# Two-layer hybrid decoder: shift sums on VectorE, a new pace for the modulation rows, and two FFN panels held back into attention

## The chip, the core and the metric

The kernel runs on one core of one Trainium2 chip. The metric is device time in microseconds (us) from one launch, the median of several runs. Instructions go to five engines: TensorE (PE in the profile, with weight loads as PEld), VectorE (DVE), ScalarE (ACT), GpSimd (POOL) and SyncE (SP), each of which works through its own queue in order.

## The reference

The input is x of 1024 tokens by 1024 channels and a conditioning vector c. Each layer makes six modulation vectors of 1024 values from c; each normalised input is scaled and shifted by two of them, and each sub-layer's output is scaled by a third before it is added to x.

```python
cond = silu(c)
for i in range(2):
    sh1, sc1, g1, sh2, sc2, g2 = split(cond @ ada_w[i] + ada_b[i], 6)
    h = rmsnorm(x, norm_mix_g[i]) * (1 + sc1) + sh1
    x = x + g1 * (rglru_mixer(h) if i == 0 else dsa_mixer(h))
    h = rmsnorm(x, norm_ffn_g[i]) * (1 + sc2) + sh2
    x = x + g2 * (square(relu(h @ ffn_w1[i])) @ ffn_w2[i])
```

Layer 0's mixer projects h to 1280 channels of a convolution branch and 1280 of a gate branch, runs a gated linear recurrence in 5 blocks of 256 channels over time, and projects back. Layer 1's mixer is attention of 16 heads with one shared key and value; an indexer of 8 heads chooses the 256 best keys for each query. The FFN is 1024 to 4096 to 1024.

## The kernel before

Activations lie with channels on the 128 partitions and tokens along the free axis, in two halves of 512 tokens, h = 0 and 1; a half of x is 8 tiles of 128 x 512. Every large product is made of three matmuls (`mm3`, L351 to L353): weights and activations are each split into a rounded part and a remainder (wh and wl, hh and hl). ScalarE rounds the weights (L328), and GpSimd or VectorE takes the remainder (L334). Layer 0's last eight FFN weight panels are written back to HBM in split form when half 0 uses them, and are only loaded for half 1.

The program text is one long list. A planner of the framework puts instructions on the engines' queues by its own estimate of when each is ready, with the place in the program as priority, so an instruction can stand in its queue ahead of one that the program names earlier. Buffers are given out by the same planner.

**Start (`startup`, L496).** For each of 8 channel blocks kt the 128 columns of the first scale and of the first shift are needed (`A0`, `S0`). Two raw tiles of `ada_w` hold both. `cols` (L555) makes the scale sums on TensorE by 8 tiny matmuls of one output column, each of which stands in the trace as two records. For kt under `NS` = 4 it makes the shift sums in the same way; for kt of 4 and above `mac` (L542) makes them on VectorE, as 8 operations of 128 x 128, which TensorE turns (L565) and VectorE reduces (L567); L568 then writes S0. The block's normalised input follows (L97 to L100), and with it the first 18 matmuls of the mixer. `lru_params` (L386) makes some 30 tiny constants of the recurrence; the program calls it in `mixer0` after the second convolution.

**Layer 0's mixer (`mixer0`, L609).** After the start it goes through a list of steps, `plan`: "c20" is the convolution (`conv`) of block 2 for half 0, "g" the gate, "l" the recurrence (`lru`), "o010" the output projection of blocks 0 and 1 for half 0. After every step `pump` takes one item from a list of small work, `fill`. Its items are the other modulation rows: `ada` (L430) gives for each row 8 `mac` items, of two VectorE operations on 128 x 512 each (L456 for the first, L458 for the others), and a `fin` that turns and reduces the sums (L465, L466). Each `mac` also starts the load of the next one's data, on ScalarE's queue (L441). The row for g1, `ada(0, 2)`, comes first; its `fin` is the eighth step of the plan, ahead of "o010", the first that needs it. Two items are pumped before the mixer. `nB` (L1321) and `nA` (L1325) make a normalised input in one step: `bc` (L84) broadcasts 1/rms over the partitions into a bank of PSUM, and `apply` runs L102 on VectorE, L103 on ScalarE and L104 on VectorE for each of 8 blocks. Output projections take one PSUM tile (`ps`, four of them) per block of 128 channels, which VectorE empties (L728).

**From layer 0 to layer 1 (`run`, L1403 on).** Half 1's second eight FFN panels run in a loop: `f1` of panel p+1, then `f2` of panel p, 8 PSUM tiles of 6 matmuls, each added to x by VectorE (L174). Between them stand blocks of layer 1 for half 0: keys, values and indexer, the scores, and `q_group(0, 0)`, the first eight heads' queries. After the last panel come half 1's norm (`stat`, L71, and `bc`), and `q_group(0, 1)` with half 1's `apply` in its gaps. Then `attention(0)` starts, which at certain points takes steps from a generator, `background`, at a given `rate` per point: half 1's keys, values and indexer, and the first half of the output projection. What is left of it when attention ends runs bare (`finish`).

Of the kernel before, what the change touches and what calls it, by code (L numbers as in the profile page):

```python
# [19 lines left out]
KT = 8  # L20
# [182 lines left out]
class Trunk:  # L203
# [292 lines left out]
    def startup(self, pool, norm, normb):  # L496


        nc, V, A = self.nc, self.nc.vector, self.nc.scalar
        NS = 4  # L500
        A0 = self.mod[0, 1] = self.const.tile([P, KT], FT, name="mod01")
        S0 = self.mod[0, 0] = self.const.tile([P, KT], FT, name="mod00")

# [10 lines left out]
        norm.bc(keep=self.nlong())  # L514
        b1 = self.small([P, KT], "mb", 1)
        V.scalar_tensor_tensor(b1, self.ada_b(0, 1), 1.0, self.gmix(0), op0=OP.add, op1=OP.mult)
        pd = [self.pd(), self.pd()]
        acc = [pd[0][:, 0], pd[0][:, 1], pd[1][:, 0], pd[1][:, 1], self.ps(), self.ps()]
        wt, ad = {}, {}
# [22 lines left out]
        def mac(kt):  # L542

            if kt < NS:
                return
# [9 lines left out]
        def cols(kt):  # L555
            ps = self.ps()
            for e in range(2 if kt < NS else 1):
                for k in range(KT):
# [4 lines left out]
            t = ps[:, 1:2]  # L563
            if kt >= NS:
                nc.tensor.transpose(ps[:, P:2 * P], sums[kt], self.ident)  # L565
# [43 lines left out]
    def mixer0(self, hx, g1, tail, first, plan):  # L609
# [21 lines left out]
        def conv(u, h, pss=None):  # L631
            pss = pss or proj(wcols(u * 256), h)
            for j in range(2):
                f = 2 * u + j
                y = self.tmp("xc")
                A.activation(y, pss[j], AF.Identity, bias=self.convb(f), scale=self.convw(3, f))
                if h == 0:
                    A.copy(halo[:, f], pss[j][:, HT - 3:HT])
                for k in range(3):
                    d = 3 - k  # L640
                    V.scalar_tensor_tensor(y[:, d:], pss[j][:, 0:HT - d], self.convw(k, f), y[:, d:],  # L641
                                           op0=OP.mult, op1=OP.add)
                if h:
                    V.tensor_tensor(y[:, 0:3], y[:, 0:3], edge[:, f], op=OP.add)
                yh, yl = self.tileR(), self.tileR()
                A.copy(yh, y)
                G.tensor_tensor(yl, y, yh.bitcast(FT), op=OP.subtract)
                xc[u, j], xcs[u, j] = y, (yh, yl)
# [83 lines left out]
        conv(0, 0, first[0])  # L732
        gate(0, 0, first[1])
        conv(1, 0, first[2])
        self.lru_params()
        for k, step in enumerate(plan):
            if callable(step):
                step()
            else:
                us = [int(u) for u in step[1:-1]]  # L740
                {"c": conv, "g": gate, "l": lru, "o": oproj}[step[0]](us if step[0] == "o" else us[0], int(step[-1]))
                if step == "c40":
                    edges()
            self.pump()


    def l1_consts(self):
# [510 lines left out]
    def run(self):  # L1258
        tc = self.tc
        mod = self.mod = {}  # L1260
        N = {}
        hm, hf = {}, {}

        def pool(st, name, bufs):
            return st.enter_context(tc.tile_pool(name=name, bufs=bufs))

        def sqs(key):
            def tail(h, m):
                if m == 0:
                    N[key, h] = Norm(self, h)  # L1270
                N[key, h].sq(m)
            return tail

        turns = []
# [5 lines left out]
        def run(gen):  # L1280
            for _ in gen:
                pass
# [8 lines left out]
        def turn_next():  # L1291
            for g in turns.pop(0):
                g()

        def flush():
            while turns:
                turn_next()
# [3 lines left out]
        NJ = 8  # L1301
# [11 lines left out]
        F = FFN(self, 0, None, hf)  # L1313
        with ExitStack() as st:
            self.tp = pool(st, "tmp0", 18)
            macs, fin = self.ada(0, 2)
            self.fill += macs
            self.ada_fill([(0, 4, self.gffn(0)), (0, 3), (0, 5)])
            self.pump(2)

            def nB():  # L1321
                N["m0", 1].bc()
                hm[1] = N["m0", 1].apply(mod[0, 1], mod[0, 0])

            def nA():  # L1325
                N["f0", 0].bc()
                hf[0] = N["f0", 0].apply(mod[0, 4], mod[0, 3])

            def stat0():
                N["f0", 0].stat()  # L1330

            def f1a():
                self.drain()
                F.load1(0)
                F.f1(0, 0)

            def f1b():
                def bcB():
                    N["f0", 1].bc()
                    hf[1] = N["f0", 1].apply(mod[0, 4], mod[0, 3])  # L1340

                F.load1(1)
                F.f1(1, 0, mid={4: lambda: N["f0", 1].stat(), 6: bcB})

            plan = [lambda: self.second(), "g10", "l00", "c20", "l10", "g20", "c30", fin, "o010", "l20", "g30", "c40",
                    "l30", "g40", nB, "o20", "l40", "c01", "g01", "o340", "l01", "c11", stat0, "g11", "c21", "l11",
                    "g21", "c31", "o011", "l21", "g31", "c41", "l31", "g41", nA, "o21", "l41", f1a, "o341", f1b]
            self.mixer0(hm, lambda: mod[0, 2], sqs("f0"), first, plan)
            self.drain()


            F.g2, F.tail = mod[0, 5], tail
            self.ada_fill([(1, 1, self.gmix(1)), (1, 0), (1, 2), (1, 4, self.gffn(1)), (1, 3), (1, 5)])
            F.load2(0, 0)
            f2 = F.f2_steps([0], 0)
            for _ in range(4):
                next(f2)
            F.f1(0, 1), F.f1(1, 1)
            F.load2(0, 1)
            run(f2)  # L1360
            F.f2([0], 1)
            for p in range(NJ):
                if p:
                    F.load2(p, 0), F.load2(p, 1)
                    for h in range(2):
                        F.f2([p], h)
                if p + 2 < NJ:
                    F.load1(p + 2)
                    F.f1(p + 2, 0), F.f1(p + 2, 1)
            self.drain()  # L1370
            F.twice = range(NJ, F.NP)
            F.single(0, NJ)
# [6 lines left out]
        with ExitStack() as st:  # L1379
            self.tp = pool(st, "tmpt", 12)  # L1380
            self.hidpool = self.tp
            self.qi, self.qiT, self.qT, self.sc = {}, {}, {}, {}
            hm[0] = []
            def start():
                N["m1", 0].bc()
                hm[0] += N["m1", 0].apply(mod[1, 1], mod[1, 0])
                self.l1_consts()

            def idx(t):
                flush()  # L1390
                for f in self.idx_steps(t):
                    f()
                self.fill += self.topk_steps(t)

            N["m1", 0].stat()
            self.npump = 2
            F.load1(NJ)
            F.f1(NJ, 1)
            start()
            blocks = [lambda: (steps(self.kv_steps(0, hm[0]), 4), steps(self.qi_steps(0, hm[0]), 4)),  # L1400
                      lambda: (idx(2), idx(3)), lambda: None, lambda: None, lambda: None,
                      lambda: (flush(), run(self.q_group(0, 0, hm[0], turns)))]
            for p in range(NJ, F.NP):  # L1403
                if p + 1 < F.NP:
                    F.load1(p + 1)
                    F.f1(p + 1, 1)
                F.load2(p, 0), F.load2(p, 1)
                F.f2([p], 1)
                if blocks:
                    blocks.pop(0)()  # L1410
            self.hidpool = None
            N["m1", 1].stat()
            flush()


            self.lo = [1, 1, 0]
            q1 = self.q_group(0, 1, hm[0], self.late_turns)
            hm[1] = []
            next(q1)
            N["m1", 1].bc(keep=self.rstd_b)  # L1420
            for k in range(KT):
                hm[1].append(N["m1", 1].apply1(k, mod[1, 1], mod[1, 0]))
                next(q1)
            run(q1)
            self.drain()

            def background():
                self.second_half()
                yield from feed(self.kv_steps(1, hm[1]), 2)
                yield from feed(self.qi_steps(1, hm[1]), 2)  # L1430
                self.reload(0)
                while self.units < 8 + 1:
                    yield
                yield from self.proj_out(0, mod[1, 2], 0)

            self.banks(True)
            self.bg, self.rate = background(), 1
            self.attention(0)
            self.finish()
            flush()  # L1440
        with ExitStack() as st:
# [27 lines left out]
            F = FFN(self, 1, mod[1, 5], hf)  # L1469
# [7 lines left out]
            f2 = F.f2_steps([F.NP - 2, F.NP - 1], 0)  # L1477
# [75 lines left out]
```

## Time and profile before

| | |
|---|---|
| time, median of 3 runs | 2583.12 us (2579.7 to 2590.5) |
| time of the profiled execution | 2589.09 us |
| its span, first to last instruction | 2587.3 us |
| TensorE busy | 2449.9 us, 95% of the span |
| VectorE busy | 1500.7 us, 58% |
| ScalarE busy | 1234.9 us, 48% |
| GpSimd busy | 965.9 us, 37% |
| mean granted TensorE clock | 0.974 of full |
| DMA | 342.53 MB, 132 GB/s over the span |

The profiled execution took 1.8 us more than its span. Busy time of TensorE is modelled for pipelined matmuls, so a slice in which it is full can still run at the lower of its two clocks. In a row of the timeline or of a view of waits the bracket at the end says how long the engine sat idle before that instruction and what released it.

### The profile page before, as it was taken

What the parts mean: (1) busy time and instruction counts of PE and PEld (TensorE: products, weight loads), DVE (VectorE), ACT (ScalarE), POOL (GpSimd) and SP (SyncE); (2) the same over time, 40 slices, a digit from 0 to 9 for tenths busy, and PEclk for the clock granted to TensorE, in tenths of its full rate; (3) what the DMA queues carried; (4) which work ended last, traced back from release to release, by engine and by line L of the source; (5) the groups of instructions that cost most, each with busy time, mean ns of one, the idle gap of its engine ahead of it and who ended that gap; (6) DMA issues with size and microseconds to landing.
All of it is one profiled execution on the core that took longest, in us unless ns stands there. A gap on an engine that the chain in (4) does not pass through costs nothing. (4 is left out here: it accounts for less than half of the span.)

```text
span 2587.3 us, 31024 instructions
## 1 busy us (share of the span) xinstructions
PE 2449.9 (95%) x11014; PEld 1976.0 (76%) x11014; DVE 1500.7 (58%) x2802; ACT 1234.9 (48%) x2187; POOL 965.9 (37%) x575
## 2 busy tenths in 40 slices
PE   8779899998999999999997999999998999999999
PEld 7567678776788888888776877888887777788887
DVE  3677965678934421366677877565558876321112
ACT  3455555632122142235546767768743974433322
POOL 3455421122221234230136932222225994344442
PEclk8889999999999999999998999999999999999999
DMA  6556466336611277744431431232330104322231
GB/s 207 197 183 202 164 220 227 123 110 212 207 49 49 98 249 284 279 165 175 147 117 31 172 102 57 91 97 82 105 131 8 34 25 144 111 96 92 88 101 62
DMA packets 212285, 342.53 MB, mean 132 GB/s; under 512 B 19658, under 2 KB 123298, under 8 KB 212130
## 3 DMA queue, kind: packets, MB, share of 16 engines
q1 hardware_dynamic: 183184, 295.29, 33.8%
q10 hardware_dynamic: 28946, 45.27, 5.3%
q8 instruction: 86, 1.41, 0.2%
q14 instruction: 69, 0.57, 0.1%
HBM read 274.97 MB, written 65.54 MB: 132 GB/s over the span
## 5 line engine op out<-in xcount | busy, mean ns | idle before, releaser
L334 POOL TENSOR_TENSOR wl<-raw,wh 128x1024 fp32r<-128x1024 f32 (+2 forms) x233 | 569.3, 2451 | 1102.3 <-ACT wh L328 1075.0
L328 ACT CAST wh<-raw 128x1024 fp32r<-128x1024 f32 (+2 forms) x296 | 305.5, 1035 | 599.9 <-PE ps L352 237.9
L351 PE MATMUL ps<-a,wh 128*128 128x512 f32 x1152 | 463.2, 405 | 20.3 <-DVE a L728 10.8
L352 PE MATMUL ps<-a,wh 128*128 128x512 f32 x1152 | 460.7, 400 | 1.3 <-POOL a L710 1.1
L353 PE MATMUL ps<-a,wl 128*128 128x512 f32 x1152 | 459.0, 399 | 0.8 <-DMA wl<-part 0.8
L351 PE MATMUL pd<-a,wh 128*128 128x512 f32 x1072 | 430.4, 402 | 18.8 <-DVE xc L641 14.2
L352 PE MATMUL pd<-a,wh 128*128 128x512 f32 x1072 | 430.8, 402 | 5.6 <-DVE a L100 3.6
L353 PE MATMUL pd<-a,wl 128*128 128x512 f32 x1072 | 429.9, 401 | 0.0
L174 DVE SCALAR_TENSOR_TENSOR a<-ps,mod,a 128x512 f32<-128x512 f32 x352 | 260.0, 747 | 262.3 <-PE ps L353 261.5
L351 PEld LDWEIGHTS ps<-a,wh 128*128 128x128 f32 x1152 | 219.4, 191 | 76.7 <-DVE a L728 11.4
L352 PEld LDWEIGHTS ps<-a,wh 128*128 128x128 f32 x1152 | 219.5, 191 | 55.3 <-POOL a L710 3.4
L353 PEld LDWEIGHTS ps<-a,wl 128*128 128x128 f32 x1152 | 219.1, 190 | 54.6 <-DMA wl<-part 1.6
L351 PEld LDWEIGHTS pd<-a,wh 128*128 128x128 f32 x1072 | 203.8, 190 | 69.9 <-issue 15.9
L352 PEld LDWEIGHTS pd<-a,wh 128*128 128x128 f32 x1072 | 204.8, 191 | 57.4 <-DVE a L100 4.6
L353 PEld LDWEIGHTS pd<-a,wl 128*128 128x128 f32 x1072 | 204.6, 191 | 49.3
L1147 POOL TENSOR_SCALAR s<-s,rr 128x128 f32<-128x128 f32 (+7 forms) x128 | 225.4, 1776 | 33.3 <-DVE rr L1145 30.1
L351 PE MATMUL ps<-hid,wh 128*128 128x512 f32 x512 | 205.0, 400 | 9.3 <-DVE a L174 6.5
L352 PE MATMUL ps<-hid,wh 128*128 128x512 f32 x512 | 203.9, 398 | 0.0
L353 PE MATMUL ps<-hid,wl 128*128 128x512 f32 x512 | 203.7, 398 | 0.0
L1025 ACT ACTIVATE signs<-sc,tc 128x384 int8<-128x384 f32 (+5 forms) x186 | 164.3, 884 | 77.5 <-DVE tc L1040 66.3
L458 DVE SCALAR_TENSOR_TENSOR a<-a,cond,a 128x512 f32<-128x512 f32 x140 | 134.7, 994 | 34.5 <-DMA a<-in_ada_w_dram 34.3
L152 DVE TENSOR_TENSOR a<-r,a 128x512 fp32r<-128x512 f32 x64 | 47.1, 757 | 140.2 <-ACT a L151 138.9
(275 smaller groups left out, 3750.9 us busy)
## 6 DMA issues: line engine op xcount, KB each, us to landing
raw<-in_ffn_w_dram SPq DMA_DIRECT2D x192, 512.0 KB, 3.7
a<-in_ada_w_dram ACTq DMA_DIRECT2D x160, 256.0 KB, 3.2
part<-wl SPq DMA_DIRECT2D x69, 512.0 KB, 3.1
wl<-part SPq DMA_DIRECT2D x69, 512.0 KB, 4.2
part<-wh SPq DMA_DIRECT2D x40, 512.0 KB, 4.1
wh<-part SPq DMA_DIRECT2D x40, 512.0 KB, 3.9
raw<-in_a_w_in_dram SPq DMA_DIRECT2D x34, 512.0 KB, 5.0
raw<-in_a_w_out_dram SPq DMA_DIRECT2D x20, 512.0 KB, 4.2
```

The source lines that it names most:

```text
L152: nc.any.tensor_tensor(ql, r, qh.bitcast(FT), op=OP.subtract)
L174: nc.vector.scalar_tensor_tensor(xt, ps, self.g2[:, m:m + 1], xt, op0=OP.mult, op1=OP.add)
L328: nc.scalar.copy(wh, raw)
L334: eng.tensor_tensor(wl, raw, wh.bitcast(FT), op=OP.subtract)
L351: pe.matmul(out, wh, xh, start=start, stop=False)
L352: pe.matmul(out, wh, xl, start=False, stop=False)
L353: pe.matmul(out, wl, xh, start=False, stop=stop)
L458: nc.vector.scalar_tensor_tensor(a, r, s, a, op0=OP.mult, op1=OP.add)
L1025: A.activation(self.signs[:, 0:L], sc, AF.Sign, bias=0.0 if neg is None else neg.bitcast(FT), accum_out=n)
L1147: G.tensor_scalar(sl[e][:, 0:L], sl[e][:, 0:L], r[:, e:e + 1], None, op0=OP.mult)
```

## The change

The shift sums of all eight blocks are made on VectorE (`NS` = 0). `lru_params` is called before the sums of the start. Ahead of the mixer no `mac` is pumped, only the first load is started; two items in place of one are pumped after steps 1, 2 and 3 of the plan. `nB` and `nA` are each cut in two: `bc` stands where the whole stood, and `apply` one step later, behind the output projection "o20" or "o21".

In the second part the loop over panels ends two panels earlier. The hidden values of panel 14 and 15 go to another pool. `q_group(0, 0)` follows the last `f1`; the `f2` of panels 14 and 15 becomes one, with 8 PSUM tiles of 12 matmuls; two of the eight run ahead of `q_group(0, 1)`, and the other six are the first steps of attention's background, at rate 0.5, followed by half 1's norm and `apply`. Then the rate goes to 1 and the old background follows.

```diff
-        NS = 4
+        NS = 0
...
         V.scalar_tensor_tensor(b1, self.ada_b(0, 1), 1.0, self.gmix(0), op0=OP.add, op1=OP.mult)
+        self.lru_params()
...
         conv(1, 0, first[2])
-        self.lru_params()
...
-            self.pump()
+            self.pump(2 if k in (1, 2, 3) else 1)
...
-            self.pump(2)
+            self.loads.pop(0)()
             def nB():
-                N["m0", 1].bc()
                 hm[1] = N["m0", 1].apply(mod[0, 1], mod[0, 0])
             def nA():
+                hf[0] = N["f0", 0].apply(mod[0, 4], mod[0, 3])
+
+            def bA():
                 N["f0", 0].bc()
-                hf[0] = N["f0", 0].apply(mod[0, 4], mod[0, 3])
...
-                    "l30", "g40", nB, "o20", "l40", ...
-                    ... "l31", "g41", nA, "o21", "l41", f1a, "o341", f1b]
+                    "l30", "g40", lambda: N["m0", 1].bc(), "o20", nB, "l40", ...
+                    ... "l31", "g41", bA, "o21", nA, "l41", f1a, "o341", f1b]
...
-                      lambda: (idx(2), idx(3)), lambda: None, lambda: None, lambda: None,
-                      lambda: (flush(), run(self.q_group(0, 0, hm[0], turns)))]
-            for p in range(NJ, F.NP):
-                if p + 1 < F.NP:
-                    F.load1(p + 1)
-                    F.f1(p + 1, 1)
+                      lambda: (idx(2), idx(3))]
+            for p in range(NJ, F.NP - 2):
+                if p + 1 == F.NP - 2:
+                    self.hidpool = None
+                F.load1(p + 1)
+                F.f1(p + 1, 1)
                 F.load2(p, 0), F.load2(p, 1)
                 F.f2([p], 1)
                 if blocks:
                     blocks.pop(0)()
-            self.hidpool = None
-            N["m1", 1].stat()
+            F.load1(F.NP - 1)
+            F.f1(F.NP - 1, 1)
             flush()
+            run(self.q_group(0, 0, hm[0], turns))
+            f2 = F.f2_steps([F.NP - 2, F.NP - 1], 1, load=True)
+            next(f2), next(f2)
             self.lo = [1, 1, 0]
-            q1 = self.q_group(0, 1, hm[0], self.late_turns)
+            run(self.q_group(0, 1, hm[0], self.late_turns))
             hm[1] = []
-            next(q1)
-            N["m1", 1].bc(keep=self.rstd_b)
-            for k in range(KT):
-                hm[1].append(N["m1", 1].apply1(k, mod[1, 1], mod[1, 0]))
-                next(q1)
-            run(q1)
             self.drain()
             def background():
+                yield from f2
+                N["m1", 1].stat()
+                yield
+                N["m1", 1].bc(keep=self.rstd_b)
+                yield
+                for k in range(KT):
+                    hm[1].append(N["m1", 1].apply1(k, mod[1, 1], mod[1, 0]))
+                    yield
+                self.rate = 1
                 self.second_half()
...
-            self.bg, self.rate = background(), 1
+            self.bg, self.rate = background(), 0.5
```

## Rows read from the trace of the kernel before

**Rows 1.** The page: the span, and busy time of each engine.
```profile
span 2587.3 us, 31024 instructions
PE 2449.9 (95%) x11014; PEld 1976.0 (76%) x11014; DVE 1500.7 (58%) x2802; ACT 1234.9 (48%) x2187; POOL 965.9 (37%) x575
```
**Rows 2.** Busy time by stretch: us, PE, PEld, DVE, ACT, POOL, clock, DMA share, GB/s.
```profile
18.30:30.00 11.70, 11.70 (x67) 11.39 (x66) 1.33 (x10) 3.05 (x5) 4.07 (x4) 0.65 1.01 293
96.00:108.00 12.00, 0.20 (x1) 0.23 (x2) 8.74 (x10) 3.67 (x7) 3.61 (x2) 0.68 1.02 370
...
250.00:300.00 50.00, 40.69 (x165) 31.81 (x164) 48.35 (x53) 29.57 (x40) 22.84 (x10) 0.90 0.43 140
800.00:850.00 50.00, 50.00 (x215) 40.22 (x214) 19.30 (x25) 9.85 (x13) 12.02 (x5) 1.00 0.15 49
...
1366.20:1403.00 36.80, 22.17 (x126) 18.89 (x126) 29.06 (x106) 20.58 (x66) 28.20 (x31) 0.78 0.11 26
1403.00:1466.00 63.00, 59.93 (x376) 55.03 (x376) 52.43 (x154) 53.20 (x157) 56.14 (x62) 0.96 0.17 60
```
**Rows 3.** Timeline of TensorE at five waits: start, length, engine, line, operation, wait.
```profile
107.80 0.76 PE L351 MATMUL pd<-a,wh 128*128 128x512 f32 x1 [12.30 <-DVE xc L641]
...
185.12 1.94 PE L465 MATMUL ps<-ident,a 128*128 128x128 f32 x8 [14.11 <-DVE a L458]
...
268.87 0.79 PE L351 MATMUL ps<-a,wh 128*128 128x512 f32 x1 [8.33 <-DVE a L728]
...
485.07 0.80 PE L351 MATMUL pd<-a,wh 128*128 128x512 f32 x1 [4.53 <-ACT a L103]
...
1380.55 0.64 PE L825 MATMUL ps<-wh,a 128*128 128x328 f32 x1 [4.38 <-DVE mn L1136]
```
**Rows 4.** Timeline of the start: tiny matmuls of block 3 and 4, S0.
```profile
46.36 4.35 PE L559 MATMUL ps<-cond,st 128*128 128x1 f32 x32
...
58.91 1.84 PE L559 MATMUL ps<-cond,st 128*128 128x1 f32 x16
...
61.93 0.15 DVE L568 TENSOR_TENSOR mod<-mt,col 128x1 f32<-128x1 f32 x1
```
**Rows 5.** The shift sums on VectorE: ns min/median/max; then busy us, mean ns.
```profile
L552 DVE SCALAR_TENSOR_TENSOR ma<-st,cond,ma x28: 342/352/2368, 51.3 to 83.8; 128x128 f32<-128x128 f32 x28
...
L552 DVE SCALAR_TENSOR_TENSOR ma<-st,cond,ma 128x128 f32<-128x128 f32 x28 | 18.5, 662 | 0.7
```
**Rows 6.** Timeline of VectorE: the first constant of the recurrence.
```profile
14.01 0.17 DVE L390 TENSOR_SCALAR hb<-col 128x20 f32<-128x20 f32 x1
```
**Rows 7.** Timeline of VectorE, 98 to 105 us: the first pumped items.
```profile
98.31 0.49 DVE L456 TENSOR_SCALAR a<-a,cond 128x512 f32<-128x512 f32 x1 [2.46 <-DMA a<-in_ada_w_dram]
...
100.91 3.51 DVE L458 SCALAR_TENSOR_TENSOR a<-a,cond,a 128x512 f32<-128x512 f32 x2
```
**Rows 8.** VectorE by line, 96 to 190 us: the macs; busy us, mean ns, waits.
```profile
L458 DVE SCALAR_TENSOR_TENSOR a<-a,cond,a 128x512 f32<-128x512 f32 x14 | 16.8, 1219 | 5.0 <-DMA a<-in_ada_w_dram 5.0
```
**Rows 9.** Timeline, 163 to 188 us: seventh and eighth mac; "l10"'s last GpSimd operation.
```profile
167.34 2.88 DVE L458 SCALAR_TENSOR_TENSOR a<-a,cond,a 128x512 f32<-128x512 f32 x1
...
183.53 2.10 DVE L458 SCALAR_TENSOR_TENSOR a<-a,cond,a 128x512 f32<-128x512 f32 x2
...
183.15 1.27 POOL L710 TENSOR_TENSOR a<-hs,a 128x512 fp32r<-128x512 f32 x1
```
**Rows 10.** Timeline of VectorE, 255 to 271 us: nB's first operations, "o20"'s first release.
```profile
258.60 1.40 DVE L102 SCALAR_TENSOR_TENSOR ns<-a,mod,ps 128x512 f32<-128x512 f32 x2
...
268.08 0.74 DVE L728 SCALAR_TENSOR_TENSOR a<-ps,mod,a 128x512 f32<-128x512 f32 x1
```
**Rows 11.** VectorE by line, 1312 to 1362 us: last panels, half 1's norm and apply.
```profile
L63 DVE TENSOR_TENSOR nl<-nl,ns 128x512 f32<-128x512 f32 x7 | 7.3, 1042 | 0.2 <-ACT ns L62 0.2
L104 DVE SCALAR_TENSOR_TENSOR a<-ns,mod,a 128x512 fp32r<-128x512 f32 x8 | 7.1, 889 | 0.3
L102 DVE SCALAR_TENSOR_TENSOR ns<-a,mod,rstd_b 128x512 f32<-128x512 f32 x8 | 5.8, 745 | 2.7 <-ACT rstd_b L87 2.7
```

More of the change, by code (lines that the diff above doesn't have):

```diff
@@ L1345, in run @@
             plan = [lambda: self.second(), "g10", "l00", "c20", "l10", "g20", "c30", fin, "o010", "l20", "g30", "c40",
-                    "l30", "g40", nB, "o20", "l40", "c01", "g01", "o340", "l01", "c11", stat0, "g11", "c21", "l11",
-                    "g21", "c31", "o011", "l21", "g31", "c41", "l31", "g41", nA, "o21", "l41", f1a, "o341", f1b]
+                    "l30", "g40", lambda: N["m0", 1].bc(), "o20", nB, "l40", "c01", "g01", "o340", "l01", "c11", stat0, "g11", "c21", "l11",
+                    "g21", "c31", "o011", "l21", "g31", "c41", "l31", "g41", bA, "o21", nA, "l41", f1a, "o341", f1b]
             self.mixer0(hm, lambda: mod[0, 2], sqs("f0"), first, plan)
```

## The prediction

> **What bounds the kernel now.** I read the page first, then a table by stretches, then TensorE's waits, longest first, and then the timelines of the engines that ended them. The page says that TensorE is the bound: 2449.9 of 2587.3 us busy [rows 1], so all its idle time together is 137 us, and a change that removes no large matmul can win only from that and from the clock. The table shows where neither is lost: in the middle of the FFN TensorE is full at full clock, 215 matmuls of 128x512 in 50 us, 0.2326 us each [rows 2]. The loss is in a few places, all of which the change touches: the start, where the granted clock was 0.65 [rows 2]; waits of 12.30 us up to 107.80 and 14.11 us up to 185.12, both ended by VectorE; 8.33 us up to 268.87 and 4.53 us up to 485.07, beside the two steps that apply a norm [rows 3]; and the beginning of the first attention, where TensorE worked 22.17 of 36.8 us at a clock of 0.78 [rows 2], with a wait of 4.38 us for VectorE in it [rows 3].
>
> The reader should also see the other side. VectorE was busy 8.74 of 12 us beside the first wait, 48.35 of 50 from 250 to 300 us, and 29.06 of 36.8 and then 52.43 of 63 us in the first attention [rows 2]. Where TensorE waits, VectorE is mostly full. The change takes nothing large from VectorE; it reorders it. So I count less than the length of each wait.
>
> **Part 1, shift sums.** It removes 8 tiny matmuls, 16 records, in each of blocks 0 to 3: 64 records, at 4.35/32 = 0.136 or 1.84/16 = 0.115 us each [rows 4] 7.4 to 8.7 us of TensorE. It adds to VectorE 32 operations of 128x128: 11 us at the median 0.352, 21 us at the mean 0.662 [rows 5], in a stretch where VectorE was busy 1.33 of 11.7 us while DMA was full at 1.01 [rows 2]. So VectorE has the room, and the data come no earlier. What counts is when S0 is there. As block 4 does it already, S0 ends at 62.08, which is 1.33 us after the last of its 16 records at 60.75 [rows 4], against 16 records more, 1.84 to 2.2 us, in the old way. That is under 1 us a block while the sums are done beside the scale's records, and a loss when they are not: 8 times 0.662 is 5.3 us a block, against 4.35 for both sums on TensorE [rows 4, 5]. Four blocks: -8 us if TensorE's time decides, +4 if VectorE does. I take -2, as the loads decide most of it.
>
> The spread of that price has its cause in the trace: the same operation took 342 ns at least and 2368 at most [rows 5]. [...]
>
> `lru_params` I cost at 0, with bounds of plus and minus 1 us: the planner has already put its first operation at 14.01 us [rows 6], though the program names it far later, and its operations run in gaps that the loads leave.
>
> **Part 2, the pace.** Four operations of two macs stand in VectorE's queue ahead of the second half of the first convolution. They wait 2.46 us for data and end at 104.42 [rows 7]; the convolution behind them frees the PSUM tile for which TensorE waits to 107.80 [rows 3]. They leave this place, so from 95.85, where VectorE began to wait, to 104.42 8.5 of the 12.30 us can go. Their loads go too, three of four, while DMA is full at 1.02 [rows 2]. But the work comes back: six more operations, these four and the eighth mac's two, must be done before the row's `fin`, at 0.75 us alone or at the mean of 1.219 [rows 8], 4.5 to 7.3 us; I take 5.9. That leaves 2.6 us.
>
> The second wait: the turns of `fin` stood in TensorE's queue until the eighth mac ended, at 185.63 (183.53 and 2.10). In the new pace the eighth comes one step earlier, in the place of the present seventh, whose last operation ended at 170.22 [rows 9]. TensorE then stops one step further on: "o010" needs the last remainder of "l10", which GpSimd ended at 184.42 [rows 9]. TensorE reached "o010" at about 187 (185.12 and 1.94 for the turns), so this alone wins 2.6 us, and with 2.6 us from the first wait 5.2. Where TensorE waits less the clock falls for less time (0.68 in the stretch of the first wait [rows 2]). Six matmuls of "o010" that need only block 0 fit into what is left of the wait, 1.4 us, and for the clock I add as much again: -8. The ends are -20 (8.5 and most of 14.11) and 0 (all given back to VectorE).
>
> **Part 3, bc and apply apart.** At 258.60 VectorE ran two operations of `apply`, 1.40 us, while the first blocks of "o20" were ready to be emptied; the first release came only at 268.08 [rows 10], behind the scan of "l30". With `apply` later, two releases take that place; two freed tiles feed 2 x 6 matmuls, 2.8 us at 0.2326. The wait of 8.33 us loses 3, and that of 4.53 up to 2, by the same reasoning. Against it stands a tile that now stays taken by 1/rms while "o20" runs, three left of four, as in the wait itself, and VectorE at 48.35 of 50 us, which pays any gain back later in "c01". I take -4, from -12 (both waits) to +2.
>
> **Part 4, held-back products.** The six PSUM tiles moved into attention are 72 matmuls, 16.7 us at 0.2326 [rows 2]. They need nothing from VectorE but 6 emptyings, and their weights come from HBM already split. They meet 14.6 idle us (36.8 less 22.17) and a clock of 0.78 [rows 2]. Attention issues nine half-units at once before its first transposes (its eight slots), a point each, so at rate 0.5 four or five tiles, 11 to 14 us, meet the gap. Against it: the norm and `apply`, 7.3 + 7.1 + 5.8 = 20.2 us of VectorE [rows 11], move in as well, where VectorE had 7.7 + 10.6 = 18.3 us free in 99.8 [rows 2]. Eight emptyings of 0.74 us fewer (12 matmuls to a tile, not 6) give 6 us back. The keys of half 1 start later, and some 24 steps of the output projection, 72 matmuls, are left for `finish`, which costs nothing as such: the same matmuls, moved behind. Bounds: -18 (idle 14.6 and the clock) and +8 (VectorE over its room by 20.2 + 4.4 - 18.3 = 6, and a late start of the keys). I take -7, under half of the idle time.
>
> The sum is -2 - 8 - 4 - 7 = -21 us on the profiled execution of 2589.1 us, 2568. That execution is 6.0 us above the median of 2583.1, so I give 2562.
>
> **Rivals.** *The stalls only move.* VectorE, not the order, bounds 96 to 350 us; what TensorE wins at 107 and 185 it waits out behind the next scan. For it: 48.35 of 50 us, and macs of 1.219 us mean [rows 2, 8]. Against it: 8.74 of 12 us includes waiting for data that need not be waited for there. Parts 2 and 3 shrink to -3, with -2 and -5 for the others: -10, 2573. [...]
>
> *The planner has done it already.* As with `lru_params` [rows 6], the order on the engines is not the program's, and the new pace gives nearly the same queues; only part 4 acts. For it: macs stand already mixed with other work [rows 7, 9]. Against it: the waits above come from places that priority fixed. -7 and -1: 2575.
>
> *The gains add up.* Both long waits go (-20), the apply steps give -8, and attention's gap fills with the clock back (-17): -45, 2538.
>
> *Slower: VectorE decides the first attention.* If its busy share there can't pass the present 52.43/63 = 0.83 [rows 2], its 81.5 us in the first 99.8 and the 20.2 + 4.4 us that come in take 128 us, 28 more; the 16.7 us of matmuls taken out ahead of attention come back bare behind it as what is left for `finish`. +28, less the 14 of the first three parts: 2597. It decides as soon as that share stays under some 0.9. Against it: half of VectorE's idle time there is waiting for ScalarE and TensorE, which more work can fill.
>
> **How the numbers follow.** Forecast 0.48; the gains add up 0.14; the stalls only move 0.16; planner 0.11; slower 0.11. From forecast and gains added up it reaches 2538 to 2575, and the range takes in the two small cases and the mild half of the slow one: 2537 to 2590. The forecast's own range is 2548 to 2574. A measurement of this kernel can tell about 0.5%, 13 us. Faster by more than that (under 2570): 0.92 of the forecast, all of the gains added up, a quarter and a tenth of the small cases, 0.63. Slower by more (over 2596): most of the last rival and a little of each other, 0.11. The rest, 0.26.
>
> **What would show it.** Part 1: no L559 run of 32 records, L552 64 operations, S0 of block 3 no later against its loads. Part 2: no L456 between the first convolution's operations, TensorE's wait there near 4 us; no wait of L465 near 185, but one of L351 for L710 of a few us. Part 3: L728 ahead of L102 behind the broadcast, and the wait there halved. Part 4: TensorE over 0.8 busy in the first 37 us of attention at a clock above 0.9, then a bare run of output projection matmuls at its end. I would be wrong if the start grew, if c01 waited for half 1's apply, or if VectorE's share stayed at 0.83 and attention grew by more than the panels that moved in.

## The result and the profile after

The changed kernel took 2607.2 us (median of 4; 2605.7 to 2611.7) beside 2585.7 us for the kernel before (median of 4): a ratio of 1.0075 [1.0058, 1.0093]. I had forecast 2562, a ratio of 0.992 to the 2583.1 known then, with a range up to 2590. It is slower, by some 20 us: 21.5 by the two medians, 19 by the ratio. The ratios here and below are those on record, with 95% intervals; they are not the quotients of the two medians.

The page, to compare with [rows 1]:

```profile
span 2603.9 us, 30949 instructions
PE 2443.4 (94%) x10954; PEld 1970.2 (76%) x10954; DVE 1519.9 (58%) x2829; ACT 1232.1 (47%) x2188; POOL 963.6 (37%) x575
```

TensorE works 6.5 us less than before and the span is 16.6 us longer, so its idle time went from 137 to 160.5 us. Where? First the busy time by stretch (columns as in [rows 2]), the first attention cut from its own start, 1347.90:

```profile
84.00:96.00 12.00, 8.21 (x30) 6.48 (x29) 7.10 (x11) 7.33 (x15) 5.52 (x4) 0.78 0.96 353
96.00:108.00 12.00, 12.00 (x62) 9.99 (x62) 6.45 (x12) 8.41 (x22) 3.61 (x4) 0.94 0.29 89
...
1347.90:1384.70 36.80, 32.17 (x165) 26.85 (x166) 23.36 (x74) 23.98 (x64) 23.81 (x24) 0.87 0.23 73
1384.70:1447.70 63.00, 50.44 (x287) 42.36 (x288) 45.77 (x143) 43.51 (x126) 39.25 (x47) 0.89 0.06 17
```

The front is better: the first wait ends at 93.54 us, in the first of these rows, and the 12 us in which TensorE stood still before are full at 0.94. The first matmul of layer 1's keys (L825) starts at 1116.9 us, before at 1129.3: 12.4 us won. One trace is a rough measure of this: the fourteen traces with parts 1 to 3 (this one and those of runs below) put it between 1112.8 and 1120.1, and the two with the front of before at 1125.7 and 1129.3. Attention's first 37 us are fuller, 32.17 in place of 22.17, as forecast, though at a clock of 0.87 where I had asked for over 0.9; but the 63 us behind them hold 287 matmuls in place of 376 [rows 2], and VectorE is busy 69.1 of the 99.8 us, before 81.5. Then TensorE's waits in sums: engine and line, releaser, total us, times, longest. For 60 to 120, 120 to 200, 200 to 330 and 1300 to 1400 us:

```profile
PE pd L351 <- ACT g L667: 3.8, 1, 3.8
...
PE ps L351 <- ACT a L710: 8.3, 1, 8.3
PE pd L351 <- DVE xc L642: 5.2, 1, 5.2
...
PE ps L351 <- DVE a L729: 13.6, 5, 8.0
...
PE ps L1124 <- ACT a L879: 21.1, 3, 19.9
```

Three of these stand where 12.30, 14.11 and 8.33 us stood [rows 3] (from the startup to the end of layer 0's mixer, lines of this kernel are one higher: L729 is L728 of before). The wait for L642 is taken up below. The last is new: at the first score matmul TensorE waits 19.87 us for ScalarE's copy of turned queries (L879). The timelines of ScalarE and of TensorE there:

```profile
1337.88 0.71 ACT L865 CAST a<-q 128x256 fp32r<-128x256 f32 x2 [8.59 <-DVE q L813]
...
1346.66 0.71 ACT L865 CAST a<-q 128x256 fp32r<-128x256 f32 x2 [2.22 <-DVE q L813]
1347.28 1.06 ACT L879 CAST a<-ps 128x512 fp32r<-128x512 f32 x2
```
```profile
1327.20 0.85 PE L874 MATMUL ps<-identR,a 128*128 128x128 f32 x8 [1.30 <-ACT q L955]
1347.91 0.47 PE L1124 MATMUL ps<-a,a 128*128 128x128 f32 x1 [19.87 <-ACT a L879]
```

TensorE turned the first queries at 1327.20, and their copy could have followed at about 1328; ScalarE sat idle from 1329.3. The copy ran at 1347.28, because in ScalarE's queue it stood behind the head splits of the second eight heads (L865), and these wait for VectorE's rope (L813; two more pairs of L865 stand between the rows shown, each behind 2.22 us). The held-back products that were to fill TensorE's time stand behind the first score matmul in TensorE's queue, and did not start there. The trace shows it for both engines: L879 stayed behind the eight L865, while ScalarE sat idle 8.59 us and three times 2.22 us, and for 19.87 us no held-back product passed the score matmul, though the first of them started at 1349.68 without a wait of its own.

### The profile page after: what moved, and what is told of

Its sections match the earlier page's. It is cut to its first block, busy times and chain, and to the rows that moved or that the text cites. A ratio compares the mean times of both kernels' runs of the same rounds, so it can differ in the third digit from the quotient of the medians.

```text
span 2603.9 us, 30949 instructions
## 1 busy us (share of the span) xinstructions
PE 2443.4 (94%) x10954; PEld 1970.2 (76%) x10954; DVE 1519.9 (58%) x2829; ACT 1232.1 (47%) x2188; POOL 963.6 (37%) x575
## 5 line engine op out<-in xcount | busy, mean ns | idle before, releaser
L351 PE MATMUL ps<-a,wh 128*128 128x512 f32 x1184 | 476.8, 405 | 28.5 <-DVE a L729 14.1
L352 PE MATMUL ps<-a,wh 128*128 128x512 f32 x1184 | 474.6, 401 | 1.5 <-POOL a L711 1.5
L353 PE MATMUL ps<-a,wl 128*128 128x512 f32 x1184 | 473.7, 400 | 1.2 <-DMA wl<-part 1.2
L174 DVE SCALAR_TENSOR_TENSOR a<-ps,mod,a 128x512 f32<-128x512 f32 x344 | 254.3, 746 | 269.0 <-PE ps L353 268.6
L351 PEld LDWEIGHTS ps<-a,wh 128*128 128x128 f32 x1184 | 226.4, 192 | 85.6 <-DVE a L729 14.8
L353 PEld LDWEIGHTS ps<-a,wl 128*128 128x128 f32 x1184 | 226.2, 191 | 56.9 <-DMA wl<-part 2.4
L352 PEld LDWEIGHTS ps<-a,wh 128*128 128x128 f32 x1184 | 226.6, 191 | 56.0 <-POOL a L711 2.8
L351 PE MATMUL ps<-hid,wh 128*128 128x512 f32 x480 | 192.5, 401 | 7.1 <-DVE a L174 4.5
L353 PE MATMUL ps<-hid,wl 128*128 128x512 f32 x480 | 191.2, 398 | 0.0
L352 PE MATMUL ps<-hid,wh 128*128 128x512 f32 x480 | 191.1, 398 | 0.0
```

The lines of the kernel that those rows point to most:

```text
L174: nc.vector.scalar_tensor_tensor(xt, ps, self.g2[:, m:m + 1], xt, op0=OP.mult, op1=OP.add)
L351: pe.matmul(out, wh, xh, start=start, stop=False)
L352: pe.matmul(out, wh, xl, start=False, stop=False)
L353: pe.matmul(out, wl, xh, start=False, stop=stop)
```

## The experiments

Each kernel was timed beside the kernel before on the same chip (medians of before 2587.9 to 2590.8 us); I compare ratios; 0.001 is 2.6 us.

**The two halves of the change.** front_only is parts 1 to 3; held_only is part 4, the diff from "blocks" on.

> The changed kernel with its last part undone: shift sums, pace and the split of bc and apply stay; the panels, the queries and the background of the first attention are as before. The first keys' matmul of layer 1 came at 1129.3 us before and at 1116.9 us after, so the first three parts should win 12.4 us: 2585.7 - 12.4 = 2573 us, 2568 to 2578, and the trace should keep the lead of some 12 us to the end. Rival: the reordering of the front also disturbs later stages (the second attention took 214.5 us before and 219.8 us after with the same text); then 2578 or more, and the lead is lost there.

> The kernel before with the last part of the change alone. By the traces the stretch from there to the end of the first attention lost 24 us, 19.9 of them in one wait of TensorE for a ScalarE copy at 1347.9 us. Expected 2585.7 + 24 = 2610 us, 2603 to 2616, with that wait at 15 to 22 us. Rival: the loss needs the front's reordering too; then nearer to 2590.

Measured: front_only 0.9961 [0.9946, 0.9975], 2576.4 us; held_only 1.0108 [1.0091, 1.0126]. The front wins 10 us of the 14 forecast (6 to 14 by the interval); part 4 loses 28.

**The queue of the turns.** turns_early is the changed kernel with the first heads' turns issued behind the matmuls of the second query projection, ahead of its ScalarE work:

```
-            run(self.q_group(0, 1, hm[0], self.late_turns))
+            q1 = self.q_group(0, 1, hm[0], self.late_turns)
+            for _ in range(KT):
+                next(q1)
+            flush()
+            run(q1)
```

turns_early_not_held issues all products of panels 14 and 15 ahead of attention as well (`run(f2)` for `next(f2), next(f2)`).

> The changed kernel with one line more: the first eight heads' queries are turned (and copied by ScalarE) after the matmuls of the second eight heads and ahead of their rotary work, as the kernel before had it, where the change leaves them to attention. Theory: ScalarE's queue holds the copies (L879) behind eight roundings of the second eight heads (L865), each of which waits for VectorE's rotary work; then 18 to 20 us come back and the time is 2583 to 2590 us, with no wait over 6 us before the first attention products. Rival: VectorE is the bound there because norm and apply moved in; then the wait only moves into attention and the time is 2598 to 2608 us.

> As the run with early turns, but all eight tiles of the last two panels' second product run ahead of the second eight heads' queries; nothing is held back, the norm and apply stay in the background. If the held-back matmuls fill idle time of the first attention, as the prediction had it, this is 5 to 15 us slower than the run with early turns. If they only change places with other filler, it is within 4 us of it.

Measured: 1.0011 [1.0, 1.0023] and 1.0008 [0.9996, 1.0021]. ScalarE now copies the turned queries at once:

```profile
1326.44 4.02 ACT L879 CAST a<-ps 128x512 fp32r<-128x512 f32 x8
```

The first score matmul starts at 1331.0 in place of 1347.9, and 0.0064 comes back, 17 us. Holding the products back is then worth nothing on balance: the two kernels can't be told apart, though in turns_early_not_held the norm and half 1's keys also begin 12 points earlier. The traces show the balance. From the first key matmul to the first score matmul it is 214.1 us with the products held back and 231.0 without, 16.9 us less, which is the 72 matmuls; from there to the first score matmul of the second attention it is 658.3 in place of 637.4, 20.9 us more. And part 4 still costs 0.005 against front_only.

**The norm of half 1.** norm_into_attention is front_only with the norm and apply moved into the background alone; norm_ahead_again is turns_early_not_held with them taken back:

```
             def background():
+                N["m1", 1].stat()
+                yield
+                N["m1", 1].bc(keep=self.rstd_b)
+                yield
+                for k in range(KT):
+                    hm[1].append(N["m1", 1].apply1(k, mod[1, 1], mod[1, 0]))
+                    yield
+                self.rate = 1
                 self.second_half()
...
-            self.bg, self.rate = background(), 1
+            self.bg, self.rate = background(), 0.5
```

> Parts 1 to 3, and of part 4 one thing alone: half 1's norm and its apply leave the gaps of the second query projection and run in the background of the first attention, at rate 0.5 until they are done. The products of panels 14 and 15, and the query projections, stay where the kernel before has them. With parts 1 to 3 alone the ratio to the kernel before was 0.9961; with part 4 and its turns brought forward it was 1.0011 (or 1.0008 with nothing held back), some 13 us more. Theory, VectorE decides the first attention: the 20.2 us of VectorE that move in, and the two trips of the norm through TensorE, are what those 13 us are; ratio 0.999 to 1.002, TensorE waiting for the norm's L63 and L79 and for L1136 in attention, and the stretch from the first score matmul to the last of attention about 15 us longer. Rival, the place does not matter: attention has room for it, and ahead of it TensorE gets the VectorE time back; ratio 0.994 to 0.998.

> The kernel with the turns brought forward and nothing held back, with half 1's norm and apply taken back to where the kernel before has them, ahead of attention in the gaps of the second query projection, and rate 1 from the start. Of part 4 it keeps the first query projection ahead of the last products, and panels 14 and 15 summed in one tile. Theory, the norm in attention is what cost the rest: ratio 0.995 to 0.998, that is about 2579 where the kernel before is 2590, with the second attention perhaps still 5 us long. Rival, the order of the query projections or the doubled tiles cost it: ratio still about 1.000.

Measured: 1.0029 [1.0018, 1.0041], so the move alone costs 0.0068, 17.6 us (the counter of the next experiment included); taken back it gives 0.9991 [0.998, 1.0002], only 0.0017 better than with the norm inside. norm_ahead_again has the norm, the pace and the counter of before, holds nothing back and has its turns early. From front_only it differs in that the first query projection stands behind the last `f1`, its turns behind the matmuls of the second one, and the products of panels 14 and 15 between the two, summed in one tile; it is still 0.003 slower, 8 us. Some of TensorE's waits there, two from the keys to attention and one from attention's beginning:

```profile
PE ps L71 <- DVE nl L63: 3.6, 1, 3.6
PE ps L84 <- DVE nl L79: 2.4, 1, 2.4
...
PE ps L874 <- DVE pl L1155: 7.1, 2, 4.9
```

The norm waits longer than in front_only, where L71 waits 2.1 us and L84 does not wait, presumably because the projection that covered it has moved. But the stretch from the first key matmul to the first score matmul, 244.2 us there and 238.1 in front_only, is also 243.1 in front_more_credit below, whose text is that of front_only there, so it shows little. Attention shows more: from its first score matmul to that of the second attention it is 629.5 us, and 623.6 to 625.5 in the seven traces that have both the order and the background of before; the turns of queries (L874) wait 7.1 us for VectorE there, 3.6 in front_only. So neither theory held as put: the places are coupled.

**The counter that attention leaves behind.** The second attention's text is unchanged, yet from its first score matmul to the first output transpose (L1249) it took 219.8 us, before 214.5. The program hands out background steps by a counter, `due`, which grows by `rate` and isn't reset. Followed through the program, it stands at 5.0 at the end of the first attention before, where the background has ended, and at 0.0 after, where rate 0.5 leaves it unfinished. The leftover lets five held-back products (tiles of the FFN panels that the program already holds back for the second attention) in at once. One line, `self.due = 0.0` (5.0, 8.0) ahead of the second attention, in front_only (0 and 8) and turns_early (5):

> Parts 1 to 3 alone, and the counter self.due set to 0 ahead of the second attention. The program's own counter stands at 5.0 there, in the kernel before and in this one (the first attention's background has ended, and five steps' worth of rate is left over); in the changed kernel it stands at 0.0, because at rate 0.5 the background does not end inside the first attention. Theory: that leftover is what the second attention lost in the changed kernel; it lets five held-back products come at the first unit, where the transposed queries are still being copied. So this kernel should show the wait of about 8.3 us of the first wide score matmul (L1124) for the copies of L879, a stretch from there to the first L1249 of about 220 to 222 us in place of 215.9, and a ratio of 0.998 to 0.9985 in place of 0.9961. Rival, the planner's state or the addresses of the tiles: no such wait, ratio 0.996.

> The changed kernel with the turns brought forward, and the counter self.due set to 5 ahead of the second attention. Theory of the leftover: the wait of 8.3 us there goes, the stretch from the first wide score matmul to the first L1249 is 215 us, ratio 0.999 (it was 1.0011 without). What is then left against parts 1 to 3 alone, some 7 to 10 us, is the norm in the first attention. Rival: ratio still 1.001.

> Parts 1 to 3 alone, and the counter set to 8 ahead of the second attention, so that all held-back products come at its first unit. If the five that come there now already cover the wait, nothing changes: ratio 0.996, within 0.001. If more cover were wanted, up to 3 us faster: 0.995. If the products are wanted later in the attention, slower, up to the 5 us of the kernel without a leftover.

Measured: 0.9978 [0.9967, 0.9989], 0.9999 [0.9989, 1.0009] and 0.9968 [0.9952, 0.9984]. TensorE's longest waits at the start of the second attention, of front_no_credit and then of turns_early_with_credit:

```profile
PE pd L1124 <- ACT a L879: 8.3, 1, 8.3
```
```profile
PE ps L874 <- DVE a L174: 2.5, 1, 2.5
```

The wait comes with the counter at 0 and goes with 5, in two kernels that differ in part 4: 0.0017 and 0.0012, 3 to 4 us. Each difference is within its noise by itself; the traces set it apart. The stretch named above is 219.0 to 222.3 us in the six with the counter at 0 and 213.7 to 217.1 in the thirteen with five or eight. Eight is no better than five.

**The norm, or its points.** empty_steps is front_only with ten empty background steps at rate 0.5 in the norm's place and the norm left ahead; empty_steps_half has them at rate 1. norm_in_at_rate_1 is norm_into_attention at rate 1, turns_early_rate_1 is turns_early_with_credit at rate 1. front_rate_up is front_only at rate 1.1. All have the counter at 5.

```
             def background():
+                for _ in range(10):
+                    yield
+                self.rate = 1
                 self.second_half()
```

> Parts 1 to 3 alone; the background of the first attention begins with ten empty steps at rate 0.5, then goes on at rate 1 as before; the counter is set to 5 ahead of the second attention. Half 1's norm stays ahead of attention: no work moves, only the keys of half 1 start 20 points later, as they do behind the norm. Theory, thin filler: what the norm in the background costs is not VectorE's time but that for 20 points the background gives TensorE no matmuls while TensorE waits for the softmax; then most of the 12 us that the norm cost in the first attention (17.6 in all, less 5 for the lost leftover) come here too, ratio 0.999 to 1.001. Rival, VectorE's load: nothing is added to VectorE, ratio 0.996 to 0.997.

> The kernel with only the norm moved into attention, at rate 1 from the start in place of 0.5, and the counter set to 5 ahead of the second attention. The norm then takes 10 points of the background in place of 20. It was 1.0029 at rate 0.5, of which some 0.002 is the lost leftover. Theory, thin filler: about half of the 12 us comes back, ratio 0.998 to 0.999. Rival, VectorE's load: the same 20.2 us of VectorE in the same stretch, only closer together, ratio 1.0005 to 1.002.

> The kernel with the turns brought forward and the counter at 5, with rate 1 from the start in place of 0.5: the six held-back tiles come within the first six points and the norm behind them, the keys of half 1 start 18 points earlier. It was 0.9999 at rate 0.5. Thin filler: the norm's points are halved, 3 to 6 us back, ratio 0.9975 to 0.999, still not under parts 1 to 3 alone (0.9961). VectorE's load: ratio 1.000, or more, since norm and softmax are closer together.

> As empty_steps, with the ten empty steps at rate 1, so that the keys of half 1 start 10 points later in place of 20. With 20 points it was 1.0009, against 0.9961 without; with the norm in the background at rate 1, 10 points late, 1.0000. If lateness alone counts, this gives the same as the norm did, 1.000; if the norm's own work has a price beside it, this comes to about half of the loss, 0.998 to 0.999, and the difference to 1.000 is that price.

> Parts 1 to 3 alone, with the background of the first attention at rate 1.1 in place of 1, and the counter set to 5 ahead of the second attention. If a thinner filler early costs, a thicker one may win a little more: ratio 0.994 to 0.996. Rival: at rate 1 TensorE has enough, and a thicker filler takes matmuls from the last units: 0.996 to 0.998.

Measured: empty_steps 1.0009 [0.9998, 1.002]; norm_in_at_rate_1 1.0 [0.9988, 1.0011]; turns_early_rate_1 1.0005 [0.9993, 1.0017]; empty_steps_half 0.9973 [0.9963, 0.9983]; front_rate_up 1.0027 [1.0018, 1.0036]. The first 100 us of the first attention, in front_only and in empty_steps:

```profile
1350.90:1450.90 100.00, 83.00 (x505) 74.32 (x505) 81.62 (x263) 74.34 (x224) 86.04 (x94) 0.90 0.15 49
```
```profile
1357.10:1457.10 100.00, 80.22 (x446) 69.04 (x446) 74.02 (x249) 68.67 (x212) 78.91 (x93) 0.86 0.13 42
```

With nothing added, only the keys of half 1 started 20 points later, TensorE does 446 matmuls in place of 505, VectorE is busy 74.0 in place of 81.6, the granted clock is 0.86 in place of 0.90, and 0.0048 is lost, 12 us. The norm at the same 20 points costs as much (1.0029, less 0.0017 for the counter). So VectorE's load is not needed for that loss. At 10 points it is: lateness alone costs 0.0012 there, no more than the noise, with the norm's work 0.0039. The two do not add up. Nor does lateness explain the changed kernel: turns_early_rate_1 starts the keys 17 points sooner than turns_early_with_credit (0.9999) and is no faster, against the expectation of thin filler. A rate of 1.1, which hands the filler out sooner, costs 0.0066, where I expected a gain or at most 0.002. Its trace shows the output projection waiting for heads that are not there yet:

```profile
PE ps L351 <- ACT a L1178: 6.4, 2, 4.7
```

In front_only this wait is 1.6 us; the difference is 5 of the 17 us, and the rest is not placed. Of the paces tried, that of before is the fastest.

**The front, part by part.** Each of parts 1 to 3 alone (part 1 without the move of `lru_params`):

> Part 1 alone: NS from 4 to 0, the shift sums of the first four blocks on VectorE; everything else as before. My forecast was -2 us (-8 to +4): ratio 0.997 to 1.0016, 0.9992 the likeliest. The first keys' matmul (L825) about 2 us earlier than before's 1129.3. [...]

> Part 2 alone: one load ahead instead of two macs ahead of the mixer, and two macs behind each of the steps 1, 2 and 3. My forecast was -8 us (-20 to 0): ratio 0.997, with the wait of 12.30 us at the first convolution down to about 4 and that of 14.11 to about 10. The rival that the stalls only move: -3, ratio 0.999. Since parts 1 to 3 together gave a ratio of 0.9961, some 10 us, this part should hold most of it if the forecast of the shares is right.

> Part 3 alone: 1/rms broadcast one step earlier than apply, for half 1 of the mixer and half 0 of the FFN. My forecast was -4 us (-12 to +2), ratio 0.9985. What the runs leave for it: parts 1 to 3 together gave 0.9961 (10 us), part 1 alone 0.9993 and part 2 alone 0.998 (7 us together), so 3 us, ratio 0.9988. The trace of the changed kernel speaks against it: the wait for L728, 8.33 us before, is not shorter there; by that it is worth nothing, ratio 1.000.

Measured: 0.9993 [0.9983, 1.0004], 0.998 [0.997, 0.999], 0.9977 [0.9964, 0.9989]: -1.8, -5.2 and -6.0 us, 13 in sum and 10 together, alike within their intervals; that of part 1 takes in zero. TensorE's longest waits, 84 to 120 and 200 to 330 us, with part 2 alone:

```profile
PE pd L351 <- DVE xc L641: 5.3, 1, 5.3
...
PE ps L351 <- DVE a L728: 13.3, 2, 12.6
```

The pace shortens the first wait from 12.30 to 5.35 us, and lengthens that of "o20" from 8.33 to 12.6; with parts 1 and 3 beside it, in front_only, it is 7.9.

## Why the prediction was wrong

**Parts 1 to 3 were right in size, not in all their steps.** The sum was -14; they measured -10 (-6 to -14 by the interval). Part 1, forecast -2, gave -1.8, which is not told apart from nothing. VectorE's price, which spoke for +4, has a row: the longest sum still took 1937 ns, against a median of 352:

```profile
L553 DVE SCALAR_TENSOR_TENSOR ma<-st,cond,ma x56: 334/352/1937, 17.0 to 70.1; 128x128 f32<-128x128 f32 x56
```

From 24.69 to 31.79 us, while GpSimd was idle, each of them took 0.34 or 0.35 us; the one at 54.56 took 1.37, beside GpSimd's L97 (54.52, 1.26 us). Eight of the 56 took over 1 us, and each of these ran beside an instruction of GpSimd; why they are longer there no run shows. But the 56 cost 28.5 us of VectorE under loads, not of the span.

Part 2, -8, gave -5.2. The first wait went as forecast, to 3.8 (5.35 with part 2 alone). The second moved from the transposes of `fin` (L465) to "o010", as forecast, and fell from 14.11 to 8.3, but not by the step that I gave: it ends with ScalarE's rounding (L710, which is L709 of before), behind the scan of "l10" on VectorE (162.25, 6.63 us), and not with GpSimd's last remainder; with part 2 alone it ends with L466, after 7.5 us. And a wait of 5.2 us for VectorE's convolution (L642) stands at 148 us; between 120 and 200 us such waits were 1.1 in all before.

Part 3, -4, gave -6, not by its step. The wait of "o20" was to be halved and is 8.0, because `apply` still stands ahead of the first release in VectorE's queue, with the scan (246.69, 4.47 us) behind it, as in [rows 10]:

```profile
244.17 1.39 DVE L102 SCALAR_TENSOR_TENSOR ns<-a,mod,ps 128x512 f32<-128x512 f32 x2
...
252.39 0.74 DVE L729 SCALAR_TENSOR_TENSOR a<-ps,mod,a 128x512 f32<-128x512 f32 x1
```

The wait of 4.53 for L103 is gone, but with part 3 alone the waits for L466 between 330 and 600 us rise from 2.3 to 6.7, so I can't place the gain.

**Part 4 is the step that failed**: forecast -7 (-18 to +8), measured 0.0114 between front_only and the whole change, +29 us, and +28 alone. In the prediction's words "They meet 14.6 idle us" and "need nothing from VectorE but 6 emptyings". They could not meet them. I listed the products and the norm that move, and left out the one line that moves with them: the first query projection now follows `flush()`, so its turns are issued inside attention. What that put behind VectorE's rope in ScalarE's queue cost 17 of the 29 us.

The runs undo the rest step by step. Letting the products go ahead gives 0.0003 (turns_early to turns_early_not_held). Taking norm, pace and counter back gives 0.0017, 4 us, together (to norm_ahead_again); of this the counter's leftover, which I did not look for and which acts 655 us behind the start of the first attention, is 3 to 4. The last 0.003, 8 us, lie between norm_ahead_again and front_only, in the new places of the first query projection, of its turns and of the last two panels' products, and in their doubled tiles. Which of these it is stays open, and no term of my sum stood for it. These shares hold for this order of undoing: "The keys of half 1 start later" stood in the prediction without a price of its own, and moved into front_only by itself that lateness costs 12 (empty_steps), the norm's whole move 17.6.

**The rivals.** The slower one had the sign, not the mechanism: VectorE's share in attention's first 99.8 us was to stay at 0.83, and it fell to 0.69. That the stalls only move is true of part 2 in part, and that the planner leaves the order as it was is true of part 3 at "o20". "A bare run of output projection" did come; whether it costs anything by itself no run shows.

The size of -7, even with the turns early, was wrong too: turns_early and turns_early_not_held differ by 0.0003. The 16.9 us that TensorE no longer worked ahead of attention came back as 20.9 behind its first score matmul, so on balance the products met no idle time.

front_only, at 0.9961, is the fastest of all kernels here by its ratio (front_more_credit, 0.9968, is not told apart from it), and beats both the kernel before and the change.

## What to carry to other kernels

Work held back to fill a gap filled nothing here while it stood in its engine's queue behind the instruction that waits (19.87 us without one held-back product), and with that wait gone it still won nothing (0.0003 between turns_early and turns_early_not_held). Before costing a moved block, list what else changes place relative to it, copies on ScalarE above all (17 of the 29 us here), and what each then queues behind. A filler that is paced by a counter hands matmuls out at fixed points: a step without matmuls, or a leftover that carries over, shifts all later ones, and in the first attention both directions cost here, 0.0048 for the keys 20 points later and 0.0066 for a rate of 1.1. Where a change has parts, price them apart; three small gains of 2 to 6 us were hidden here under one loss of 29.
